# Weights loaded twice, once rounded by GpSimd's transfers, with the remainder formed by VectorE alone

## The chip, the cores and the metric

One core of one Trainium2 chip runs the whole program. The metric is the device time of one execution in microseconds; lower is better. Before the change it is 3626.53 us, the median of three runs (3625.71 to 3627.09).

## The reference, cut to what matters

A stack of two kinds of transformer block on one sequence of 512 tokens with 1024 features, in float32. Two layers of the first kind (Fourier mixing, window attention and memory attention side by side, then a gated feed-forward layer), two of the second (a half-weighted feed-forward layer, a mixer of three branches, a second half-weighted feed-forward layer), and a last norm. The parts that the text speaks of:

```python
def swiglu(x, w1, w2):                        # four layers of it, and two of the first kind's like it
    gu = x @ w1                               # 1024 x 5632
    return (silu(gu[..., :2816]) * gu[..., 2816:]) @ w2

def hybrid_mixer(h, ...):                     # twice
    proj = h @ w_in + b_in                    # 1024 x 5792
    y_a = (rg_lru(conv4(pa1)) * gelu(pa2)) @ lru_w_out
    y_b = mla_branch(cq, ckv, kpe, ...)       # 8 heads of causal attention
    c = pc1 * sigmoid(pc2)
    c = causal_depthwise_conv(c, dw_w, dw_b)  # 31 taps on 512 channels
    y_c = silu(layer_norm(c)) @ conv_w_out + b_out
    return (g0 * y_a + g1 * y_b + g2 * y_c) @ w_out
```

## The kernel before, in words

**Tiles.** Activations lie with features along the 128 partitions and the 512 tokens along the free axis, as tiles `s` of 128 x 512 float32 from one pool of `NSLOT` = 95 slots. Weights come as tiles of 128 x 128; one load brings eight of them (512 KB) into one of `RBUFS` = 3 buffers `raw`. PSUM tiles are named `ps`.

**Three matmuls for one.** To reach float32 accuracy with the fast `fp32r` type, each operand is held as a rounded part and a remainder. `split` (line 727) makes them: `h` is a copy into `fp32r` (the profile's CAST), `l` is the source minus `h` (TENSOR_TENSOR, subtract). `mm3` (line 721) then issues three matmuls. `wload` (line 695) does this for weights: one DMA on SyncE's queue into `raw` (the very first load in two halves, flag `fresh`), and for each four weight tiles one cast and one subtraction of 128 x 512. `wsmall` (line 713) does the same for small weights, in slots.

**Who does what.** `Plan` (line 316) records all instructions in the program's order, simulates the engines with the prices of `price` (line 397) and issues each engine's instructions in the order in which the simulation started them. Some instructions may go to either of two engines, whichever the simulation finds free: `Plan.copy` (line 342) is a copy or cast on ScalarE or VectorE; `Plan.tt` (line 334) is an elementwise operation of two tensors on VectorE or, when no operand is in PSUM, on GpSimd. So weights' casts fall to ScalarE and VectorE, and remainders and other additions and products fall to VectorE and GpSimd. The order on each engine is fixed at build time; at run time each engine waits only on semaphores.

**Stages.** In order: the first block's layer (`block1`, line 1115), its feed-forward layer (`ffn`, line 952), both again; then `ffn`, `mixer` (line 1331), `ffn`, twice. Feed-forward layers are long runs of 128 x 512 matmuls. In `mixer`, `mla` (line 1517) interleaves attention heads with `filler`, which projects the two other branches; `lru` (line 1445) and `dwconv` (line 1486) are elementwise: a `dwconv` is 30 dependent SCALAR_TENSOR_TENSOR instructions on VectorE for each of four tiles, with widths from 511 down to 482, the tap's weight from `vecs`. `conv_norm` (line 1495) adds up the four results and sums over features with a matmul against `onesr`, a tile of ones; the third branch waits for it.

**GpSimd's queue** also issues the DMAs of `fourier` (line 1290), which load the tables `c_dft` into `fp32r` tiles (32 of them, 129 KB each), and computes 17 small powers (`rinv`) for norms. All recorded instructions are issued at line 647, so every row of the profile says L647.

Of the kernel before, what the change touches and what calls it, by code (L numbers as in the profile page):

```python
# [12 lines left out]
F32 = mybir.dt.float32  # L13
# [47 lines left out]
def constants():  # L61
    """Arrays that depend on shapes alone."""
# [63 lines left out]
class Pack:  # L126
    """Vectors along the features, one column for each 128 of them."""
# [114 lines left out]
class View:  # L242
    """A part of a tile that the plan has yet to place."""
# [22 lines left out]
    def box(self):  # L266
        """Partitions and columns that it spans."""
# [10 lines left out]
class Slot:  # L278
    """A tile of the plan: its pool's tag and how long it is needed."""
# [36 lines left out]
class Plan:  # L316
    """Records the instructions in the order of the program, with what each reads and writes, and
    issues them in the order in which the engines could start them: among those that are ready, an
    engine takes the one that the tensor engine needs first."""
# [14 lines left out]
    def tt(self, out, in0, in1, op):  # L334
        """An elementwise instruction that the vector engine or GpSimd may take."""
        kw = dict(out=out, in0=in0, in1=in1, op=op)
        ways = [("vector", "tensor_tensor", (), kw)]
        if not any(v.tile.psum for v in (out, in0, in1)):
            ways.append(("gpsimd", "tensor_tensor", (), kw))
        self.record(ways)  # L340

    def copy(self, out, in_):
        """A copy that the scalar or the vector engine may take."""
        kw = dict(out=out, in_=in_)
        self.record([("scalar", "copy", (), kw), ("vector", "tensor_copy", (), kw)])

    def scale(self, out, in_, by):
        """A product with a column (or a number)."""
# [48 lines left out]
    def price(self, way, outs, ins):  # L397
# [21 lines left out]
        if fn == "dma_start":  # L419
            return 1.0  # L420
# [6 lines left out]
    def schedule(self):  # L427
        """The order of issue and each instruction's engine, by a simulation of the engines."""
# [43 lines left out]
        def room(op, ahead, e):  # L472
            """Whether its tiles fit now, and still would with all before it in the program."""
# [14 lines left out]
        def elsewhere(op, e):  # L488
            """When another engine would have finished it."""
# [59 lines left out]
        while done < len(self.ops):  # L549
            moved = True  # L550
            while moved:
                moved = False
                for e in self.ENGINES:
                    while idle_at[e] <= now + 1e-9 and queues[e]:
# [21 lines left out]
                        elif op.fn == "dma_start":  # L576
                            op.end = now + 4.0
# [73 lines left out]
class Weights:  # L651
    """Tiles of weights, four in each slot."""
# [11 lines left out]
class Net:  # L664
    NSLOT = 95
    RBUFS = 3
# [3 lines left out]
    def __init__(self, plan, I, out, at, nl1=2, nl2=2):  # L670
        self.nc, self.I, self.out, self.at = plan, I, out, at
        self.nl1, self.nl2 = nl1, nl2
        self.fresh = True
# [21 lines left out]
    def wload(self, src):  # L695
        """A load of weights and the split of its tiles of 128 columns."""
# [3 lines left out]
        for c in (0, 4) if self.fresh else (0,):  # L700
            e = c + 4 if self.fresh else n
            nc.sync.dma_start(out=raw[:, c:e], in_=src[:, c:e])
        self.fresh = False
        hs, ls = [], []
        for c in range(0, n, 4):
            e = min(c + 4, n)
            h, l = (self.t(F32R)[:, :128 * (e - c)].rearrange("p (k c) -> p k c", c=128) for _ in range(2))
            self.split(raw[:, c:e], h, l)
# [4 lines left out]
    def wsmall(self, src):  # L713
        """Weights of at most 512 columns, in slots."""
        n = src.shape[1]
        raw, wh, wl = (self.t(dt)[:, :128 * n].rearrange("p (k c) -> p k c", c=128) for dt in (F32, F32R, F32R))
        self.nc.sync.dma_start(out=raw, in_=src)
        self.split(raw, wh, wl)
        return wh, wl
# [22 lines left out]
    def linear(self, srcs, acts, evac, hold=0, before=None, first=0, last=0, done=None):  # L742
        """srcs: for each m tile the pieces of its weights along K. The first hold tiles
        are evacuated after the matmuls of all of them. The first and the last tiles can go by halves
        of the tokens, so that what waits for them or for their operands can begin earlier."""
# [34 lines left out]
    def linear4(self, pairs, acts, evac, only=None):  # L780
        """K = 512, two m tiles for each load."""
# [26 lines left out]
    def norm(self, xs, d, bias=None, wide=False):  # L808
        """1/rms of xs (after their bias) in all partitions."""
# [17 lines left out]
    def wide(self, parts, d):  # L827
        """1/rms in all partitions, from sums of squares; takes less of the tensor engine
        than inv() and bcast() but longer."""
# [784 lines left out]
```

## Time and profile before

| what | us |
|---|---|
| runs of the kernel, median (range) | 3626.53 (3625.71 to 3627.09) |
| the profiled execution, from its first to its last instruction | 3625.2 |
| TensorE (PE) busy | 3460.9 (95%) |
| VectorE (DVE) busy | 2558.2 (71%) |
| ScalarE (ACT) busy | 1008.3 (28%) |
| GpSimd (POOL) busy | 735.2 (20%) |

No time of its own is given for the profiled execution beside its span of 3625.2 us; the median of the runs lies 1.3 us above the span. Busy shares are means over stages that differ: in the feed-forward layers TensorE never pauses, in the mixers VectorE hardly does. The engines' names in the rows are PE, DVE, ACT, POOL and SP (SyncE).

### The profile page before, as it was taken

The numbers are of one execution on the slowest core, as the hardware profiler recorded it, in microseconds if no ns is written. First come the engines' busy times: TensorE is split into PE (matmuls) and PEld (weight loads), VectorE is DVE, ScalarE is ACT, GpSimd is POOL, SyncE is SP. The second block draws the span as 40 slices with busy tenths as digits, with TensorE's granted clock in tenths as the row PEclk, the third lists the DMA queues.
The fourth block names the chain that finished last, engine by engine and source line by source line (L and its number), as shares of the span: only waits on it lengthen the run. The fifth ranks groups of instructions, "written<-read, shape, count | busy, mean of one in ns | idle before, by whom it ended". The sixth has DMA issues, their size and how long they took to land.

```text
span 3625.2 us, 42725 instructions
## 1 busy us (share of the span) xinstructions
PE 3460.9 (95%) x16280; PEld 2874.0 (79%) x16280; DVE 2558.2 (71%) x4377; ACT 1008.3 (28%) x1944; POOL 735.2 (20%) x582
## 2 busy tenths in 40 slices
PE   7999999989999999999995999999999999599998
PEld 6788888778888888887784888888888878488887
DVE  8987545888553865479999765566556999975553
ACT  5632112453110311037523211021102662321110
POOL 4341003443000400013434000000001243510000
PEclk8999999999999999999997999999999999899999
DMA  4223232232223232331222422332233122242231
GB/s 143 81 66 111 82 102 73 81 99 76 82 94 98 81 109 84 103 118 55 93 72 86 139 76 80 108 121 78 80 112 133 42 72 93 81 138 83 80 104 50
DMA packets 105406, 331.61 MB, mean 91 GB/s; under 512 B 12272, under 2 KB 21232, under 8 KB 105200
## 3 DMA queue, kind: packets, MB, share of 16 engines
q1 hardware_dynamic: 100592, 324.64, 27.2%
q0 software_dynamic: 4608, 4.23, 0.5%
q8 instruction: 128, 2.10, 0.2%
q14 instruction: 78, 0.64, 0.1%
HBM read 319.91 MB, written 6.29 MB: 90 GB/s over the span
## 4 chain that ended last, share of the span: by engine, by line
PE 76%; DVE 21%; issue 2%; ACT 1%; DMA 0%; POOL 0%; SPq 0%; DVEq 0%; ACTq 0%; POOLq 0%
PE ps L647 76%; DVE s L647 20%; ACT s L647 1%; DVE nb L647 0%; DMA s<-in_x 0%; DVE mx L647 0%; DMA raw<-in_a_in 0%; DVE sp L647 0%; POOL rinv L647 0%; SPq L647 0%; DVE rc L647 0%; POOL s L647 0%; DVE sums L647 0%; DVE rms L647 0%; DVEq L647 0%
## 5 line engine op out<-in xcount | busy, mean ns | idle before, releaser
L647 PE MATMUL ps<-s 128*128 128x512 f32 (+3 forms) x15706 | 3399.8, 378 | 44.9 <-DVE s L647 36.0
L647 PEld LDWEIGHTS ps<-s 128*128 128x128 f32 (+1 forms) x15706 | 2804.5, 189 | 609.1 <-DVE s L647 50.0
L647 DVE TENSOR_TENSOR s<-ps,s 128x512 f32<-128x512 f32 (+5 forms) x642 | 394.8, 635 | 515.6 <-PE ps L647 512.2
L647 DVE TENSOR_TENSOR s<-raw,s 128x512 fp32r<-128x512 f32 (+1 forms) x918 | 640.1, 719 | 23.4 <-ACT s L647 5.5
L647 POOL TENSOR_TENSOR s<-s 128x512 f32<-128x512 f32 (+2 forms) x277 | 335.1, 1219 | 1526.6 <-DVE s L647 893.2
L647 POOL TENSOR_TENSOR s<-raw,s 128x512 fp32r<-128x512 f32 (+1 forms) x250 | 366.6, 1480 | 1177.0 <-ACT s L647 534.7
L647 ACT ACTIVATE s<-s 128x512 f32<-128x512 f32 (+1 forms) x325 | 182.6, 579 | 1074.6 <-DVE s L647 1041.1
L647 DVE TENSOR_TENSOR s<-s 128x512 f32<-128x512 f32 (+3 forms) x573 | 423.9, 746 | 60.5 <-ACT s L647 35.9
L647 ACT CAST s<-raw 128x512 fp32r<-128x512 f32 (+1 forms) x564 | 326.4, 606 | 434.9 <-DMA raw<-in_b 181.1
L647 DVE SCALAR_TENSOR_TENSOR s<-s,vecs 128x256 fp32r<-128x256 f32 (+25 forms) x446 | 386.2, 897 | 2.8
L647 DVE CAST s<-raw 128x512 fp32r<-128x512 f32 (+1 forms) x604 | 277.9, 466 | 21.2 <-DMA raw<-in_b 10.9
L647 ACT ACTIVATE s<-s,vecs 128x512 f32<-128x512 f32 (+2 forms) x211 | 134.5, 654 | 389.5 <-DVE s L647 354.2
L647 DVE SCALAR_TENSOR_TENSOR s<-ps,s 128x512 f32<-128x512 f32 (+1 forms) x33 | 22.2, 674 | 236.4 <-PE ps L647 236.4
L647 ACT CAST s<-s 128x512 fp32r<-128x512 f32 (+1 forms) x97 | 58.6, 609 | 235.4 <-DVE s L647 183.2
L647 ACT ACT_TABLE_LOAD x68 | 87.2, 1283 | 54.0 <-DVE s L647 52.2
L647 DVE CAST s<-s 128x512 fp32r<-128x512 f32 (+2 forms) x167 | 87.3, 523 | 14.4 <-POOL s L647 10.6
L647 PE MATMUL ps<-ident,s 128*128 128x128 f32 x392 | 65.9, 293 | 31.0 <-DVE s L647 29.0
L647 ACT ACTIVATE s<-ps 128x512 f32<-128x512 f32 (+1 forms) x40 | 21.3, 533 | 235.6 <-PE ps L647 235.5
L647 DVE RECIPROCAL s<-s 128x128 f32<-128x128 f32 (+1 forms) x48 | 83.3, 1742 | 4.2 <-ACT s L647 4.0
L647 PE MATMUL ps<-s,onesr 128*128 128x512 f32 x36 | 13.0, 444 | 76.5 <-DVE s L647 42.3
L647 PEld LDWEIGHTS ps<-ident,s 128*128 128x128 f32 x392 | 49.3, 149 | 46.2 <-DVE s L647 34.2
L647 ACT ACTIVATE s<-s,nb 128x256 f32<-128x256 f32 (+3 forms) x128 | 70.6, 553 | 37.5 <-DVE nb L647 37.3
(61 smaller groups left out, 701.1 us busy)
## 6 DMA issues: line engine op xcount, KB each, us to landing
raw<-in_b SPq DMA_DIRECT2D x240, 512.0 KB, 3.3
raw<-in_a_f SPq DMA_DIRECT2D x120, 512.0 KB, 3.3
raw<-in_b_in SPq DMA_DIRECT2D x92, 512.0 KB, 3.2
raw<-in_b SPq DMA_DIRECT2D x32, 384.0 KB, 3.6
raw<-in_a_in SPq DMA_DIRECT2D x19, 512.0 KB, 4.2
raw<-in_a_out SPq DMA_DIRECT2D x16, 512.0 KB, 3.2
raw<-in_b_out SPq DMA_DIRECT2D x16, 512.0 KB, 3.2
raw<-in_a_f SPq DMA_DIRECT2D x16, 384.0 KB, 3.6
```

Source lines behind the costliest of these rows:

```text
L647: getattr(getattr(nc, op.eng), op.fn)(*[real(v) for v in op.args], **{k: real(v) for k, v in op.kw.items()})
```

## The change

The weights' rounded part no longer comes from a cast on ScalarE or VectorE. A second DMA, on GpSimd's queue, reads the same weights from HBM and writes them into an `fp32r` tile; the DMA converts. The raw weights still arrive on SyncE's queue, and VectorE subtracts. `Plan.tt` no longer offers GpSimd, so every elementwise operation of two tensors is VectorE's; GpSimd keeps the DMAs and the 17 powers. Two slots fewer, one raw buffer more, the first load in one piece, and the planner's prices for GpSimd's DMAs change: they now share the planner's one DMA channel with SyncE's. Since the planner picks the order by its prices, the order changes on every engine.

```diff
@@ class Plan: def tt(self, out, in0, in1, op)
-        kw = dict(out=out, in0=in0, in1=in1, op=op)
-        ways = [("vector", "tensor_tensor", (), kw)]
-        if not any(v.tile.psum for v in (out, in0, in1)):
-            ways.append(("gpsimd", "tensor_tensor", (), kw))
-        self.record(ways)
+        self.record([("vector", "tensor_tensor", (), dict(out=out, in0=in0, in1=in1, op=op))])
@@ price
         if fn == "dma_start":
-            return 1.0
+            return 0.6
@@ schedule
                         elif op.fn == "dma_start":
-                            op.end = now + 4.0
+                            n = int(np.prod(op.kw["out"].shape[1:]))
+                            passes = 2 if "accum_op" in op.kw else 1
+                            state["dma"] = max(state["dma"], now + 1.0) + passes * 128 * n * 4 / 330e3
+                            op.end = state["dma"] + 1.6
@@ class Net
-    NSLOT = 95
-    RBUFS = 3
+    NSLOT = 93
+    RBUFS = 4
@@ wload
-        for c in (0, 4) if self.fresh else (0,):
-            e = c + 4 if self.fresh else n
-            nc.sync.dma_start(out=raw[:, c:e], in_=src[:, c:e])
-        self.fresh = False
+        nc.sync.dma_start(out=raw, in_=src)
         hs, ls = [], []
         for c in range(0, n, 4):
             e = min(c + 4, n)
             h, l = (self.t(F32R)[:, :128 * (e - c)].rearrange("p (k c) -> p k c", c=128) for _ in range(2))
-            self.split(raw[:, c:e], h, l)
+            nc.gpsimd.dma_start(out=h, in_=src[:, c:e])
+            nc.tt(l, raw[:, c:e], h, ALU.subtract)
@@ wsmall
         self.nc.sync.dma_start(out=raw, in_=src)
-        self.split(raw, wh, wl)
-        return wh, wl
+        self.nc.gpsimd.dma_start(out=h, in_=src)
+        self.nc.tt(l, raw, h, ALU.subtract)
+        return h, l
```

How the built programs differ. In the whole program VectorE has 4379 instructions before and 4279 after, ScalarE 1786 and 1214, GpSimd 587 and 1256 (1247 of them DMAs, 1215 of weights), TensorE 16199 in both.

GpSimd's queue in the first mixer, where the second and third branches are computed (`raw` is a weight buffer, `s` a slot), before:

```order
L647 TENSOR_TENSOR s_16391<-raw_16332,s_16384 128x512
L647 TENSOR_TENSOR s_16428<-raw_16332,s_16411 128x512
L647 TENSOR_TENSOR s_16470<-raw_16372,s_16449 128x512
L647 TENSOR_TENSOR s_16533<-raw_16430,s_16509 128x512
L647 TENSOR_TENSOR s_15911<-s_15911,s_16480 128x512
L647 TENSOR_TENSOR s_16562<-raw_16472,s_16555 128x512
```

and of the change (`in_b_mo0`, `in_b_in0` are weights in HBM):

```order
L646 DMA s_15860<-in_b_mo0 128x512
L646 DMA s_15868<-in_b_mo0 128x512
L646 DMA s_15923<-in_b_in0 128x512
L646 DMA s_15940<-in_b_in0 128x512
L646 DMA s_15963<-in_b_in0 128x512
L646 DMA s_15983<-in_b_in0 128x512
```

Remainders and additions have left this queue, and DMAs stand there instead.

VectorE's queue at the end of the first mixer's `dwconv` and the start of `conv_norm`, before:

```order
L647 SCALAR_TENSOR_TENSOR s<-s,vecs 128x483
L647 TENSOR_TENSOR s<-ps,s 128x512
L647 SCALAR_TENSOR_TENSOR s<-s,vecs 128x482
L647 TENSOR_TENSOR s<-s 128x512 x2
L647 TENSOR_TENSOR s<-ps,s 128x512
L647 TENSOR_TENSOR s<-s 128x512
L647 TENSOR_TENSOR s<-raw,s 128x512 x2
```

and of the change:

```order
L646 SCALAR_TENSOR_TENSOR s<-s,vecs 128x483
L646 SCALAR_TENSOR_TENSOR s<-s,vecs 128x482
L646 TENSOR_TENSOR s<-s 128x512 x5
L646 TENSOR_TENSOR s<-raw,s 128x512 x2
L646 TENSOR_TENSOR s<-s 128x512 x13
L646 TENSOR_TENSOR s<-ps,s 128x512
```

The two orders do much the same work around the last tap; between the first SCALAR_TENSOR_TENSOR of `mla` and this last tap VectorE has 508 instructions before and 557 after (76 remainders of weights for 26, 60 other two-tensor operations in SBUF for 37, 55 scalings for 48, no cast of weights for 21, 20 other casts for 31).

TensorE at the same place, before (`onesr` is the tile of ones of `conv_norm`):

```order
L647 MATMUL ps<-s 128x512 x583
L647 MATMUL ps<-s,onesr 128x512 x2
L647 MATMUL ps<-s 128x512 x31
L647 MATMUL ps<-s,onesr 128x512 x2
L647 MATMUL ps<-s 128x512 x535
```

and of the change:

```order
L646 MATMUL ps<-s 128x512 x584
L646 MATMUL ps<-s,onesr 128x512 x2
L646 MATMUL ps<-s 128x512 x23
L646 MATMUL ps<-s,onesr 128x512 x2
L646 MATMUL ps<-s 128x512 x525
```

Counted from the program's start, 8909 matmuls stand ahead of the first `onesr` pair before and 8927 after; in the second mixer 14070 and 14081.

## Rows read from the trace of the kernel before

**Rows 1.** The page: busy time by engine, and the chain by engine.

```profile
PE 3460.9 (95%) x16280; PEld 2874.0 (79%) x16280; DVE 2558.2 (71%) x4377; ACT 1008.3 (28%) x1944; POOL 735.2 (20%) x582
PE 76%; DVE 21%; issue 2%; ACT 1%; DMA 0%; POOL 0%; SPq 0%; DVEq 0%; ACTq 0%; POOLq 0%
```

**Rows 2.** Windows: a feed-forward stretch, first mixer, second mixer, a turn, the start.

```profile
core 0: us, PE busy (x) PEld busy (x) DVE busy (x) ACT busy (x) POOL busy (x), PEclk, DMA share, GB/s
2084.00:2628.00 544.00, 544.00 (x2402) 450.62 (x2401) 308.54 (x529) 80.56 (x135) 25.82 (x18) 1.00 0.28 90
...
1599.00:1933.00 334.00, 295.26 (x1362) 239.54 (x1360) 324.12 (x541) 152.70 (x281) 127.03 (x85) 0.95 0.20 67
2806.00:3137.00 331.00, 294.90 (x1367) 239.33 (x1365) 322.92 (x542) 152.97 (x282) 130.20 (x85) 0.96 0.20 68
...
619.00:663.00 44.00, 38.09 (x233) 34.16 (x233) 41.22 (x54) 17.58 (x38) 27.95 (x26) 0.92 0.37 125
...
0.00:11.00 11.00, 4.32 (x8) 2.38 (x9) 5.72 (x12) 5.67 (x8) 0.20 (x4) 1.00 0.76 241
11.00:53.00 42.00, 33.98 (x144) 27.71 (x143) 41.62 (x51) 22.34 (x39) 23.62 (x18) 0.95 0.50 176
```

**Rows 3.** Timeline of TensorE at `conv_norm`, first and second mixer.

```profile
1936.39 1.22 PE L647 MATMUL ps<-s,onesr 128*128 128x512 f32 x2 [35.26 <-DVE s L647]
...
3141.56 1.22 PE L647 MATMUL ps<-s,onesr 128*128 128x512 f32 x2 [34.22 <-POOL s L647]
```

**Rows 4.** Timeline of 1910 to 1922, VectorE and GpSimd: start, length, instructions.

```profile
1910.50 0.68 DVE L647 TENSOR_TENSOR s<-ps,s 128x512 f32<-128x512 f32 x1
1911.10 9.61 DVE L647 SCALAR_TENSOR_TENSOR s<-s,vecs 128x482 f32<-128x482 f32 x7
1911.95 1.62 POOL L647 TENSOR_TENSOR s<-s 128x512 f32<-128x512 f32 x1 [1.89 <-DVE s L647]
1913.53 1.69 POOL L647 TENSOR_TENSOR s<-raw,s 128x512 fp32r<-128x512 f32 x1
1915.19 1.69 POOL L647 TENSOR_TENSOR s<-s 128x512 f32<-128x512 f32 x1
```

**Rows 5.** VectorE's groups in the first mixer, 1599 to 1933: busy us, mean ns.

```profile
L647 DVE SCALAR_TENSOR_TENSOR s<-s,vecs 128x509 f32<-128x509 f32 (+29 forms) x147 | 138.4, 972 | 0.9
...
L647 DVE TENSOR_TENSOR s<-raw,s 128x512 fp32r<-128x512 f32 x26 | 20.7, 804 | 0.0
L647 DVE TENSOR_TENSOR s<-s 128x512 fp32r<-128x512 f32 (+2 forms) x25 | 19.4, 777 | 0.2
...
L647 DVE SCALAR_TENSOR_TENSOR s<-s 128x512 f32<-128x512 f32 x16 | 14.1, 882 | 0.0
L647 DVE CAST s<-ps 128x384 fp32r<-128x384 f32 (+4 forms) x19 | 10.1, 547 | 3.4 <-PE ps L647 3.2
```

**Rows 6.** The same window by form: two widths of `dwconv` that GpSimd left alone.

```profile
L647 DVE SCALAR_TENSOR_TENSOR s<-s,vecs 128x508 f32<-128x508 f32 x4 | 2.9, 736 | 0.0
...
L647 DVE SCALAR_TENSOR_TENSOR s<-s,vecs 128x484 f32<-128x484 f32 x4 | 2.8, 711 | 0.0
```

**Rows 7.** All instructions on `raw`: duration ns min/median/max.

```profile
L647 DVE TENSOR_TENSOR s<-raw,s x918: 414/684/1785, 5.8 to 3570.6; 128x512 fp32r<-128x512 f32 x175, 128x256 fp32r<-128x256 f32 x9
L647 DVE CAST s<-raw x604: 280/419/1527, 14.0 to 3569.8; 128x512 fp32r<-128x512 f32 x143, 128x256 fp32r<-128x256 f32 x8
...
DMA to landing us min/median/max: 3.0/3.3/7.4
```

**Rows 8.** The converting DMAs of GpSimd's queue today, and the page's queues.

```profile
L647 POOL DMA_DIRECT2D s<-in_c_dft x32: 527/567/755, 157.7 to 770.5; - x32
...
DMA to landing us min/median/max: 2.3/2.6/4.2
...
q1 hardware_dynamic: 100592, 324.64, 27.2%
q0 software_dynamic: 4608, 4.23, 0.5%
```

**Rows 9.** VectorE's groups in the turn 619 to 663.

```profile
L647 DVE TENSOR_TENSOR s<-raw,s 128x512 fp32r<-128x512 f32 x15 | 13.1, 912 | 0.1
L647 DVE SCALAR_TENSOR_TENSOR s<-s,vecs 128x256 fp32r<-128x256 f32 x11 | 9.1, 878 | 0.0
```

**Rows 10.** The chain at the start: the input's last tile.

```profile
4.50 6.77 DMA s<-in_x
```

More of the change, by code (lines that the diff above doesn't have):

```diff
@@ L672, in __init__ @@
         self.nl1, self.nl2 = nl1, nl2
-        self.fresh = True
     def t(self, dt=F32):
@@ L715, in wsmall @@
         n = src.shape[1]
-        raw, wh, wl = (self.t(dt)[:, :128 * n].rearrange("p (k c) -> p k c", c=128) for dt in (F32, F32R, F32R))
+        raw, h, l = (self.t(dt)[:, :128 * n].rearrange("p (k c) -> p k c", c=128) for dt in (F32, F32R, F32R))
         self.nc.sync.dma_start(out=raw, in_=src)
-        self.split(raw, wh, wl)
-        return wh, wl
+        self.nc.gpsimd.dma_start(out=h, in_=src)
+        self.nc.tt(l, raw, h, ALU.subtract)
+        return h, l
     def mm3(self, ps, wh, wl, ah, al, start, stop, **k):
```

## The prediction

> **What bounds the kernel now.** I read the page first: TensorE is busy 95% of the span and carries 76% of the chain, VectorE 21% [rows 1]. The windows then separate the stages [rows 2]. In the feed-forward stretch TensorE is busy all 544 us, 2402 matmuls at 226 ns; VectorE is busy 57% of it, GpSimd 26 us. Nothing that VectorE, ScalarE or GpSimd save there can shorten the run. In the two mixers it is the other way round: VectorE is busy 324.1 of 334 us and 322.9 of 331 us (97%), while TensorE stands 39 and 36 us. The timeline shows where: ahead of the `onesr` matmul of `conv_norm` TensorE waits 35.3 us in the first mixer and 34.2 us in the second [rows 3], for the end of the depthwise convolution and the sum over it. The second of these waits is ended by a GpSimd instruction. So the change is worth what it does to VectorE in the mixers, plus the few turns between stages where VectorE is also full (41.2 of 44 us, [rows 2]).
>
> **What the reader should see next: GpSimd slows VectorE.** From 1911.95 on GpSimd runs its two-tensor instructions back to back, and beside them seven convolution taps of VectorE take 9.61 us, 1.37 us each [rows 4]; taps that GpSimd left alone take 711 to 736 ns [rows 6]. A remainder has a median of 684 ns and a maximum of 1785 ns; a cast 419 and 1527 ns [rows 7]. An instruction of VectorE that meets one on GpSimd thus loses about what it takes itself. GpSimd is busy 127 and 130 us in the mixers [rows 2].
>
> **The sum, part by part.**
>
> *Mixers, what goes.* In the first mixer 147 taps and the like average 972 ns; at 730 ns (between the two rows of [rows 6]) that is 147 x 0.242 = 35.6 us less. 26 remainders at 804 against 684: 3.1. 25 other two-tensor operations at 777 against 684: 2.3. 16 of SCALAR_TENSOR_TENSOR on slots at 882 against 684 (taken from the remainder, also two tensors in SBUF): 3.2. These four groups [rows 5, 6, 7] give 44 us; the smaller groups I leave out as a reserve.
>
> *Mixers, what comes.* By the order, up to the last tap VectorE has 50 remainders and 23 other two-tensor operations more, 73 x 0.684 = 49.9 us; one more evacuation, 0.7; 7 scalings at about a cast's 0.419, 2.9. It has 21 casts of weights less, 8.8 us; 2 other SBUF casts less, 0.8; 9 casts out of PSUM less at 0.547 [rows 5], 4.9. Net 39.0 us.
>
> So VectorE reaches the last tap 5 us earlier. The order also puts 18 matmuls more (11 in the second mixer) ahead of the wait; at 0.226 us they are 4.1 and 2.5 us of TensorE's standing time filled. I take 9 and 8 us: **17 us for both mixers**. The second is taken as the first's mirror, its VectorE and GpSimd times differing by 1% and 2% [rows 2].
>
> *Turns.* At 619 to 663, 15 remainders average 912 ns and 11 half-width splits 878 [rows 9]; at 684 and half a tap's width, say 475, they lose 3.4 + 4.4 us, and the smaller groups about as much again. The order gives this turn 15 instructions more on VectorE, 6 to 7 us after the casts that go. I take **7 us** for this turn and, since TensorE stands little at the two later turns into feed-forward layers, 3 us for those together.
>
> *Casts and ScalarE.* ScalarE loses its weights' casts and is busy 28% [rows 1]: nothing on the path. In feed-forward layers VectorE loses about 85 casts and gains some 10 to 40 two-tensor operations per layer: hidden under TensorE; if that cover went, it would be a gain of some us.
>
> *DMA traffic.* The rounded copies are 536 loads of 512 KB, 48 of 384 KB and 6 MB of small ones, 306 MB. At SyncE's rate (27.2% for 324.64 MB) they add 26% of the 16 DMA engines, at the present converting DMAs' rate (0.5% for 4.23 MB, rows of half the length) 36% [rows 8]: 53 to 63% in all. Hidden: 24 matmuls take 5.4 us, and that is the time for one raw load and two copies.
>
> *GpSimd's queue.* 1247 DMAs x 0.567 us = 707 us [rows 8], as busy as today, one copy per 2.7 us needed. In the order each copy waits for the copy eight places ahead, so eight may be under way; at 4.2 us of landing, the slowest seen, that allows one per 0.5 us. The 17 powers stand in the same queue behind copies that wait for a free slot; I cost that at nothing, since the slots come free in the order in which TensorE uses them, with the bound in the third rival.
>
> *Start.* The input's last tile lands at 11.3 us [rows 10] at 241 GB/s with DMA 76% busy [rows 2]. The copies begin at once on the other queue: between 0 and a doubling of that 6.8 us. Against it, VectorE, full from 11 to 53 us (41.6 of 42, [rows 2]), loses GpSimd's company (23.6 us busy) and has 45 instead of 55 instructions up to the first evacuation. But TensorE has 89 instead of 140 matmuls by then. I take 0 within -8 and +12.
>
> Sum: 17 + 7 + 3 + 0 = 27, and 8 for the groups left out as a reserve in the two mixers (5 casts, scalings and additions each that sit beside GpSimd, and `conv_norm` itself, 20 of whose 28 us have GpSimd beside them): **35 us**. The execution read has a span of 3625.2 us; the runs' median is 1.3 above. 3626.5 - 35 = **3592 us**. Its own range, from half to one and a half times the gain: 3570 to 3612.
>
> **A rule against it.** The converting DMAs of today took 527 to 755 ns to issue and 2.3 to 4.2 us to land while VectorE worked beside them [rows 8], so the sum prices no hold-up. The Trainium skill (SBUF — State Buffer, "A bandwidth-pool intuition that's wrong" and "Who interferes with whom") says that a DMA issued by GpSimd cannot write its descriptors while VectorE copies or casts in its two-port mode, about 3.1 us instead of 0.62. No run so far shows that length. By it, an estimate: if one in ten of 102 copies per mixer met such an instruction and lost 2.5 us on VectorE's path, 50 us in all, the result would be 3642 instead of 3592.
>
> **Rivals.**
>
> 1. *More than forecast, 3555.* All of TensorE's standing in the mixers that is above what the fill needs goes: half of 39 + 36 us. For it: 130 us of GpSimd beside VectorE may cost more than my four groups say. Against: 39 us of new work per mixer.
> 2. *No gain, 3626.* VectorE stays the bound of the mixers, and the 39 us that come equal what goes, because its instructions are slowed by the descriptors' writing as they were by arithmetic, or the start takes the gain back. For it: the margin of the mixers is only 5 us of 330. Against: operations beside today's 32 DMAs kept their usual length.
> 3. *Slower: the copy comes after its remainder's turn, 3670.* VectorE works in order, and each remainder now waits for two transfers, one of them issued by a queue whose head may wait for a slot. Everything behind it on VectorE, taps too, waits along. The place is the mixers, where VectorE has no slack. A landing spreads by 1.6 us on GpSimd's queue and 4.1 us on SyncE's (median to maximum, [rows 7, 8]). If 19 of the 76 remainders came 2 us late, that is 38 us per mixer: 3592 + 76 = 3668. It decides from about 9 us of such waits per mixer on, since the gain there is 9. For it: only 2.6 to 3.3 us separate issue from use at best, and twice the bytes share 16 engines. Against: the DMA engines are 20% busy in the mixers [rows 2], and copies can be issued long ahead.
> 4. *VectorE's own work holds GpSimd's issue up, 3656.* The place is the 102 copies of each mixer: a copy whose issue meets a cast or a scaling of VectorE lands late. Today's landings spread from 2.6 to 4.2 us, 1.6 us [rows 8]; if one copy in five comes so much later on VectorE's path, 20 x 1.6 = 32 us per mixer, 64 in all: 3592 + 64 = 3656. For it: VectorE is busy 97% there, so that most issues have something beside them. Against: the longest issue of today is 755 ns, and the weights' casts leave VectorE. This is the Trainium skill's rule named above, at a price from rows.
>
> **How the numbers follow.** A measurement of this kernel can tell 0.2%, 7 us, from no change. Chances: forecast 0.48, rival 1 0.09, rival 2 0.13, rival 3 0.23, rival 4 0.07. Faster is the forecast and rival 1, 0.57; same is rival 2, 0.13; slower rivals 3 and 4, 0.30. The range for 8 in 10 runs from 3548, which takes in most of rival 1, to 3690, which takes in rival 4 and rival 3 up to some 24 late copies per mixer.
>
> **What the changed profile would show.** Right: VectorE's remainders at 684 ns and its taps at 711 to 736 ns throughout the mixers; GpSimd without two-tensor rows but the powers; the wait ahead of `onesr` at 20 to 28 us; feed-forward stretches still without a pause of TensorE; DMA share near 0.55 there. Wrong, if VectorE's idle time in the mixers is ended by DMAs into `s` or `raw`, if TensorE pauses in a feed-forward layer, or if the remainders stay near 800 ns with GpSimd doing no arithmetic.

## The result, and the profile after

The changed kernel takes **3589.18 us** (median of 4 runs, 3586.07 to 3589.67); the kernel before took 3626.81 in the same session. The ratio is 0.9895 with a 95% interval of 0.9881 to 0.9909: faster by 37.6 us, 33 to 43 by the interval. 3592 had been forecast. The profiled execution has a span of 3587.8 us against 3625.2, and 37.4 us less is what has to be found in the rows.

The page after, busy times by engine and the chain by engine (answers to [rows 1]):

```profile
PE 3463.5 (97%) x16280; PEld 2874.5 (80%) x16280; DVE 2312.7 (64%) x4277; ACT 699.4 (19%) x1372; POOL 671.1 (19%) x1251
PE 87%; DVE 10%; issue 1%; DMA 1%; ACT 0%; SPq 0%; POOL 0%; POOLq 0%; DVEq 0%; ACTq 0%
```

TensorE's work is what it was (2.6 us more); 40 us of its standing are gone, and VectorE's share of the chain falls from 21% to 10%. VectorE is busy 245 us less, though it has only 100 instructions fewer and these are no shorter on the whole: 604 casts of raw weights went, and 527 two-tensor operations came from GpSimd. The fall is time that instructions no longer lose.

The windows of [rows 2], over the same times, after (the changed kernel enters the two mixers 21 and 31 us earlier, so its rows there reach further into the work):

```profile
core 0: us, PE busy (x) PEld busy (x) DVE busy (x) ACT busy (x) POOL busy (x), PEclk, DMA share, GB/s
2084.00:2628.00 544.00, 544.00 (x2402) 450.46 (x2401) 261.48 (x421) 37.96 (x59) 104.90 (x199) 1.00 0.61 185
1599.00:1933.00 334.00, 300.67 (x1363) 245.36 (x1362) 322.75 (x612) 126.81 (x228) 58.99 (x110) 0.94 0.52 154
2806.00:3137.00 331.00, 296.99 (x1351) 242.83 (x1350) 319.57 (x593) 124.49 (x220) 59.90 (x112) 0.95 0.55 166
619.00:663.00 44.00, 43.69 (x287) 40.02 (x286) 41.02 (x83) 11.14 (x28) 12.36 (x24) 1.00 0.91 281
0.00:11.00 11.00, 2.79 (x5) 1.50 (x6) 5.29 (x11) 3.26 (x4) 6.20 (x15) 1.00 0.86 256
11.00:53.00 42.00, 32.99 (x118) 24.82 (x117) 31.32 (x51) 11.41 (x17) 12.71 (x23) 0.80 1.09 349
```

The feed-forward stretch is still without a pause, at a DMA share of 0.61 instead of 0.28. In the mixers VectorE is as full as before (97%), but runs 612 instructions where 541 ran. At the turn it runs 83 instead of 54, and TensorE 287 matmuls instead of 233. The last row has turned the other way: from 11 to 53 us the DMA engines are full, VectorE idles for a quarter, and TensorE has 118 matmuls instead of 144.

VectorE's groups in the first mixer, after (lines, busy us and mean ns; answers to [rows 5]):

```profile
L646 DVE SCALAR_TENSOR_TENSOR s<-s,vecs 128x511 f32<-128x511 f32 (+23 forms) x140 | 96.6, 729 | 0.7
...
L646 DVE TENSOR_TENSOR s<-raw,s 128x512 fp32r<-128x512 f32 x88 | 58.2, 681 | 0.0
L646 DVE TENSOR_TENSOR s<-s 128x512 fp32r<-128x512 f32 (+2 forms) x73 | 47.1, 672 | 0.5
...
L646 DVE SCALAR_TENSOR_TENSOR s<-s 128x512 f32<-128x512 f32 x16 | 10.9, 684 | 0.3 <-ACT s L646 0.2
```

Taps 729 ns instead of 972, remainders 681 instead of 804, other two-tensor operations 672 instead of 777, the last group 684 instead of 882. And no remainder of the whole run is slowed any more. All instructions of VectorE on `raw` (count, then ns min/median/max), where [rows 7] had 684 with a maximum of 1785:

```profile
L646 DVE TENSOR_TENSOR s<-raw,s x1168: 414/683/694, 7.5 to 3534.1; 128x512 fp32r<-128x512 f32 x195
```

At the turn of 619 to 663, the two groups of [rows 9] that took 912 and 878 ns:

```profile
L646 DVE TENSOR_TENSOR s<-raw,s 128x512 fp32r<-128x512 f32 x17 | 10.8, 682 | 0.0
L646 DVE SCALAR_TENSOR_TENSOR s<-s,vecs 128x256 fp32r<-128x256 f32 x15 | 6.5, 476 | 0.0
```

The copies of GpSimd's queue, the largest group and the one with the longest issue (ns min/median/max), and the page's two load queues ([rows 8]):

```profile
L646 POOL DMA_DIRECT2D s<-in_b x544: 527/528/652, 1140.1 to 3526.5; - x182
...
L646 POOL DMA_DIRECT2D s<-in_a_mk x8: 527/532/807, 24.8 to 149.6; - x8
```

```profile
q0 software_dynamic: 176832, 310.49, 30.9%
q1 hardware_dynamic: 100448, 324.64, 27.0%
```

TensorE's pauses at `conv_norm` in the first mixer, after (timeline of TensorE; the last bracket is the idle time ahead and who ended it):

```profile
1883.40 6.97 PE L646 MATMUL ps<-s 128*128 128x512 f32 x18 [10.65 <-DVE s L646]
...
1898.38 1.22 PE L646 MATMUL ps<-s,onesr 128*128 128x512 f32 x2 [6.43 <-DVE s L646]
...
1907.64 0.73 PE L646 MATMUL ps<-s,onesr 128*128 128x512 f32 x2 [1.34 <-DVE s L646]
...
1920.77 4.63 PE L646 MATMUL ps<-s 128*128 128x512 f32 x10 [11.93 <-DVE s L646]
```

The 35.3 us wait of [rows 3] is 6.4 now, but two others have come beside it: the 10.65 and the 11.93 us above. In the second mixer the three are 14.48, 3.16 and 11.94 us.

**Where the 37 us come from.** TensorE executes 16280 matmuls in either kernel. I take from each trace the start of the 1250th, 5000th, 7500th, 9500th and 14500th (counted from 0; all in feed-forward layers, where TensorE never pauses, so the order of single matmuls doesn't matter) and of the last. The table gives, for each stretch between two of them, its length less that of the kernel before, in us; the kernels of the experiments stand beside. Each column is one execution. How far single ones differ shows in e7, which has the changed kernel's order on VectorE, ScalarE and GpSimd up to the first mixer and yet gains 4.8 us more in the second attention block.

| stretch | changed | e1 | e3 | e5 | e9 | e6 | e7 | e2 | e10 | e8 | e11 |
|---|---|---|---|---|---|---|---|---|---|---|---|
| start, to 259 us before | +2.1 | -17.6 | -14.2 | -10.7 | -13.8 | -7.3 | +2.5 | +23.7 | -16.7 | -14.8 | -22.0 |
| second attention block, to 1036 | -17.7 | -17.2 | -25.1 | -16.9 | -16.9 | -17.1 | -22.5 | +7.7 | -16.6 | -25.1 | -9.0 |
| turn at 1194 to 1233, to 1573 | -4.9 | -5.1 | -4.9 | -5.0 | -5.0 | -5.0 | -4.9 | -0.5 | -3.0 | -4.9 | -4.9 |
| first mixer, to 2063 | -10.9 | -10.5 | -8.2 | -10.8 | -10.8 | -2.2 | -24.6 | +13.0 | +21.8 | -51.8 | -51.8 |
| second mixer, to 3227 | -5.6 | -5.3 | -2.8 | -5.5 | -5.5 | +4.1 | -19.0 | +22.0 | +27.9 | -46.1 | -46.0 |
| all, to the last matmul | -37.1 | -55.9 | -55.3 | -49.2 | -52.3 | -27.7 | -68.8 | +65.9 | +13.1 | -142.6 | -133.9 |

For the changed kernel: the second attention block gives most, the mixers 16.5, and the start takes 2.1. What the runs had to tell is whether GpSimd's arithmetic is the cause (A), or the casts that left the other engines (B), or the second transfer (C), and what goes on at the start (D or E).

### The profile page after: what moved, and what is told of

Read it like the earlier page. It is cut to its first block, busy times and chain, and to the rows that moved or that the text cites. A ratio compares the mean times of both kernels' runs of the same rounds, so it can differ in the third digit from the quotient of the medians.

```text
span 3587.8 us, 43800 instructions
## 1 busy us (share of the span) xinstructions
PE 3463.5 (97%) x16280; PEld 2874.5 (80%) x16280; DVE 2312.7 (64%) x4277; ACT 699.4 (19%) x1372; POOL 671.1 (19%) x1251
## 4 chain that ended last, share of the span: by engine, by line
PE 87%; DVE 10%; issue 1%; DMA 1%; ACT 0%; SPq 0%; POOL 0%; POOLq 0%; DVEq 0%; ACTq 0%
PE ps L646 87%; DVE s L646 10%; ACT s L646 0%; DMA s<-in_pos 0%; DMA s<-in_x 0%; DVE sp L646 0%; SPq L646 0%; ACT L646 0%; DVE nb L646 0%; DVE mx L646 0%; DVE rc L646 0%; POOLq L1594 0%; POOL rinv L646 0%; DVE rms L646 0%; POOL s L646 0%
## 5 line engine op out<-in xcount | busy, mean ns | idle before, releaser
L646 PE MATMUL ps<-s 128*128 128x512 f32 (+4 forms) x15706 | 3406.6, 378 | 99.1 <-DVE s L646 88.1
L646 PEld LDWEIGHTS ps<-s 128*128 128x128 f32 (+2 forms) x15706 | 2805.1, 189 | 672.8 <-DVE s L646 105.7
L646 DVE TENSOR_TENSOR s<-ps,s 128x512 f32<-128x512 f32 (+4 forms) x642 | 397.7, 636 | 639.5 <-PE ps L646 634.1
L646 DVE TENSOR_TENSOR s<-raw,s 128x512 fp32r<-128x512 f32 (+1 forms) x1168 | 736.7, 672 | 59.5 <-DMA raw<-in_b 13.7
L646 DVE TENSOR_TENSOR s<-s 128x512 f32<-128x512 f32 (+3 forms) x850 | 515.2, 624 | 44.4 <-ACT s L646 22.1
L646 POOL DMA_DIRECT2D s<-in_b x544 | 287.5, 534 | 1302.1 <-PE ps L646 940.0
L646 DVE SCALAR_TENSOR_TENSOR s<-s,vecs 128x256 fp32r<-128x256 f32 (+25 forms) x446 | 286.6, 677 | 2.8 <-ACT s L646 0.4
L646 POOL DMA_DIRECT2D s<-in_a_f x272 | 144.2, 538 | 561.0 <-PE ps L646 385.7
L646 POOL DMA_DIRECT2D s<-in_b_in x184 | 99.2, 541 | 396.5 <-PE ps L646 310.7
L646 ACT CAST s<-ps 128x256 fp32r<-128x256 f32 (+4 forms) x154 | 66.2, 458 | 89.9 <-PE ps L646 73.6
```

The lines of the kernel that those rows point to most:

```text
L646: getattr(getattr(nc, op.eng), op.fn)(*[real(v) for v in op.args], **{k: real(v) for k, v in op.kw.items()})
```

## The experiments

Each ratio is against the kernel before in the same session.

**e1_vector_only.** The kernel before, with GpSimd's arithmetic taken away and nothing else:

```diff
-        ways = [("vector", "tensor_tensor", (), kw)]
-        if not any(v.tile.psum for v in (out, in0, in1)):
-            ways.append(("gpsimd", "tensor_tensor", (), kw))
-        self.record(ways)
+        self.record([("vector", "tensor_tensor", (), kw)])
```

> The kernel before with one edit: two-tensor operations have VectorE as their only engine. Weights are still loaded once and cast by ScalarE or VectorE, so no second transfer exists. Theory A (the change gains because GpSimd's two-tensor instructions stop slowing VectorE): VectorE's remainders come down to 684 ns and its taps to about 730 ns. Up to the last tap of a mixer its instructions sum to 372 us at the durations they have beside an idle GpSimd, 10 more than in the changed kernel (362) and some 12 less than the 332 plus 52 of slowing in the kernel before. So 3589 + 2 x 10, and a few us in the turns: 3612 us, between 3600 and 3622. Theory B (the gain comes from the casts that leave VectorE and ScalarE, whoever does the arithmetic): VectorE gets 411 instructions more and loses none, 40 us more per mixer, and the time is 3690 us or so; anything above 3640 speaks for B.

Measured: 3570.67 us, ratio 0.9847 (0.9834 to 0.9860). B is out: VectorE has 411 instructions more than before, and the kernel is 56 us faster. A's side, but 41 us below its point and outside its range: this one edit gives more than the whole change. Three groups of VectorE in the first mixer (lines, 1599 to 1933):

```profile
L644 DVE SCALAR_TENSOR_TENSOR s<-s,vecs 128x510 f32<-128x510 f32 (+26 forms) x136 | 93.3, 728 | 0.7
L644 DVE TENSOR_TENSOR s<-raw,s 128x512 fp32r<-128x512 f32 x99 | 65.1, 682 | 0.2
...
L644 DVE TENSOR_TENSOR s<-s 128x512 f32<-128x512 f32 (+1 forms) x72 | 47.0, 678 | 0.6
```

And its window of 11 to 53, where the changed kernel's VectorE idled and its DMA share was 1.09:

```profile
11.00:53.00 42.00, 36.47 (x158) 29.75 (x157) 40.06 (x70) 20.20 (x35) 0.00 (x0) 0.96 0.48 162
```

The durations are those of the changed kernel. By the table it gains what the changed kernel gains in every stretch, to within 0.5 us, but for the start, where it is 19.7 us ahead. So the second transfer, with the edits beside it (slots, buffers, the planner's prices), brings nothing over the old casts anywhere and costs 19.7 us at the start. My 20 us for 372 instead of 362 us of VectorE's work in the two mixers did not show: in the traces VectorE's instructions from the 7500th matmul to the first mixer's last tap sum to 364.2 us in e1 and 364.1 in the changed kernel, and that tap ends 343.3 and 343.5 us after the matmul.

**e3_scalar_cast.** The changed kernel without the second transfer; ScalarE casts:

```diff
-            nc.gpsimd.dma_start(out=h, in_=src[:, c:e])
+            nc.scalar.copy(h, raw[:, c:e])
...
-        self.nc.gpsimd.dma_start(out=h, in_=src)
+        self.nc.scalar.copy(h, raw)
```

> The changed kernel with one edit in the two loaders: the rounded weights are cast from raw by ScalarE alone, and no second transfer is made. GpSimd's queue keeps its 32 transfers and the powers. Theory A (what counts is VectorE's work and that GpSimd does no arithmetic; the second transfer only takes casts off engines that have room): VectorE sums to 367 us in each mixer, 5 more than the changed kernel, and the start is spared the traffic, 2 us by 260 us: 3597 us, between 3588 and 3605. Theory C (the second transfer is what makes it pay, because a remainder then waits for two loads side by side and not for a load, a cast and ScalarE's queue): remainders wait for ScalarE, VectorE idles in the mixers for over 10 us each, and the time is 3615 us or more.

Measured: 3571.47 us, 0.9847 (0.9834 to 0.9861). C is out, and my 3597 was too slow: I had put 2 us on the start, which gained 16.3, and nothing on the second attention block, which gained 7.4. ScalarE is busy 1321.6 us here, 37% of the span, so the casts have room there. The whole time can't be told apart from e1's, though e3 has the edits beside the second transfer and e1 has not. By the table, e3 is 2.7 and 2.8 us behind the changed kernel in the mixers, so there the second transfer gives a little over casts by ScalarE alone.

**e2_gpsimd_back.** The changed kernel with `Plan.tt` as before the change (the removed lines of e1's diff put back); the copies stay.

> The changed kernel with one edit: GpSimd may take two-tensor operations again; the rounded copies stay on its queue. VectorE's instructions up to the last tap of a mixer sum to 316 and 321 us instead of 362. Theory A: GpSimd takes 461 of them, against 527 in the kernel before, and slows VectorE by about 52 x 461/527 = 45 us per mixer, which gives the 44 us back; remainders average about 800 ns again, and the copies queue behind arithmetic: 3595 to 3630 us, 3605 the likeliest. Theory B (GpSimd's arithmetic is free help for VectorE): some 40 us per mixer less, up to the 30 us for which TensorE stands there: 3530 to 3560 us.

Measured: 3684.56 us, 1.0159 (1.0145 to 1.0173). A's side, but 80 us above its likeliest value and outside its range; the five runs spread from 3678.00 to 3693.92, and the rows are from the longest. VectorE's groups in the first mixer:

```profile
L650 DVE SCALAR_TENSOR_TENSOR s<-s,vecs 128x509 f32<-128x509 f32 (+28 forms) x115 | 97.1, 876 | 3.3 <-ACT s L650 2.7
...
L650 DVE TENSOR_TENSOR s<-raw,s 128x512 fp32r<-128x512 f32 x38 | 32.1, 853 | 2.9 <-DMA s<-in_b_in 2.9
```

From its table of waits (engine, what it waited for, us in total, times, longest):

```profile
DVE s L650 <- DMA s<-in_a_f: 63.9, 39, 3.5
POOL s L650 <- DMA raw<-in_b: 44.7, 6, 10.5
...
POOL s L650 <- DMA raw<-in_b_lo: 24.7, 3, 13.2
```

The slowing is back (876 and 853 ns), and something new with it: GpSimd stands up to 13 us in front of a remainder whose raw weights have not landed, with copies queued behind it. VectorE's waits for copies grow too, from 12.7 to 63.9 us for `in_a_f`, but 58.7 of these lie between 261 and 620 and between 860 and 1250 us, mostly feed-forward layers; in the two mixers they are 8.5 and 3.9 us, for 9.5 and 3.1 in the changed kernel. So copies do come late here, as in the third rival, but that they cost anything is not shown. How the 80 us divide between the slowing and the blocked queue I did not separate.

**e5_start16 and e9_start40.** The changed kernel; the first 16 (40) loads are cast by ScalarE instead of loaded twice:

```diff
-            nc.gpsimd.dma_start(out=h, in_=src[:, c:e])
+            if self.loads < 16:
+                nc.scalar.copy(h, raw[:, c:e])
+            else:
+                nc.gpsimd.dma_start(out=h, in_=src[:, c:e])
```

> The changed kernel with one edit: the first 16 loads of weights have their rounded part cast by ScalarE instead of loaded a second time (32 of 1215 copies fewer). In the changed kernel the DMA engines are over 90% busy from 0 to 45 us (116% and 117% from 15 to 45), the 100th matmul starts 14.0 us later than before the change, and the stretch up to the first feed-forward layer is 2.1 us behind. Theory D (the copies that run ahead crowd out the input and the first weights): the DMA share from 15 to 45 us falls below 0.9, the 100th matmul comes at about 36 us instead of 47.7, and the entry into the feed-forward layer is 3 to 9 us earlier: 3580 to 3586 us. Theory E (the start is bound by VectorE and the chain through it, and the traffic is beside it): no change beyond 2 us, 3587 to 3591 us.

> The changed kernel with the first 40 loads of weights (all of the first attention block and part of its feed-forward layers) cast by ScalarE instead of loaded a second time; with 16 it took 3577.7 us. Theory A (away from the start the second transfer costs and gives nothing: in every later stretch the changed, the vector-only and the ScalarE-cast kernels gain the same within 1 us): 3571 us, between 3568 and 3575. If the copies cost something later as well, it stays at 3576 to 3578 us.

Measured: 3577.66 us, 0.9865 (0.9852 to 0.9878), and 3573.77 us, 0.9855 (0.9842 to 0.9869). D holds, and e5 gains more than D's range gave it (3580 to 3586); e9 lies in its range. The window of 15 to 45 us in the changed kernel, then in e5 (columns as above):

```profile
15.00:45.00 30.00, 21.79 (x76) 17.07 (x76) 24.76 (x40) 8.57 (x13) 11.13 (x20) 0.72 1.16 389
```

```profile
15.00:45.00 30.00, 30.00 (x135) 24.82 (x134) 27.48 (x46) 19.17 (x34) 3.48 (x6) 1.00 0.64 220
```

The DMA share falls from 1.16 to 0.64, TensorE has no pause left where it stood 8.2 us, and the 100th matmul (counted from 0) starts at 33.8 instead of 47.7. The granted clock tells the same: 0.72 of full speed on average in the changed kernel, a mix of the levels of 1.2 and 2.4 GHz behind TensorE's pauses (0.50, which is 1.2 GHz, from 20 to 35 us), 1.00 (2.4 GHz throughout) in e5. What was late stands in the changed kernel's chain of 0 to 100 us: the last tile of the input takes 9.52 us to land, 6.77 before ([rows 10]), and the positions 11.62 us behind it (at most 5.5 before):

```profile
4.82 9.52 DMA s<-in_x
14.36 11.62 DMA s<-in_pos
```

With 40 loads the start gains 15.9 against the changed kernel, and all later stretches stay within 0.8 us of it. e9's remaining 2 to 3 us to e1 and e3 lie inside the intervals.

**e6_lead25.** All copies stay, but none is planned over 25 us ahead of its use:

```diff
+            nc.lead = 25.0
             nc.gpsimd.dma_start(out=h, in_=src[:, c:e])
+            nc.lead = nc.AHEAD
```

> The changed kernel with one edit: a rounded copy may be planned at most 25 us before TensorE needs it, instead of 120 us; nothing else about the copies changes, and all 1215 stay. Theory D1 (the start is lost because copies that nobody needs yet run ahead of the input and the first weights): the DMA share from 15 to 45 us falls from 1.16 to below 0.9 and most of the 19.7 us by which the start of the changed kernel stands behind the vector-only kernel comes back: 3570 to 3580 us. Theory D2 (the first layers need both transfers of their weights at the rate at which they come, so no order of them helps): 3585 to 3592 us. If copies that start only 25 us ahead come late, VectorE waits for transfers into the slots in the mixers too, and the time is above 3592.

Measured: 3598.97 us, 0.9923 (0.9909 to 0.9936): outside D1's and D2's ranges; it lies where late copies were expected, but not for that cause. The table splits it. The start is 9.4 us better than the changed kernel's (DMA share 0.83 from 15 to 45 us), about half of what crowding cost, where D1 wanted most of it. Yet the 100th matmul still starts at 46.1 us: thirteen copies are issued by 13.6 us as in the changed kernel, and the lead holds back only later ones. So what is lost up to there seems lost to copies that are needed early, which is nearer to D2. Against this the entry into each mixer loses: between the 7500th and the 8000th matmul 13.4 us, in the second mixer about as much. TensorE waits there 6.48 us for ScalarE, behind VectorE's instructions, at 1586.13, and at 1570 to 1610 has 116 matmuls where the changed kernel has 177 (granted clock 0.83 and 1.00). VectorE's waits for copies are not longer than in the changed kernel (10.5 us on `in_a_f` and 2.3 on `in_b_in`, for 12.7 and 12.5), so this is another order of issue and not late landings. Which step of the planner makes it, I leave open.

**e7_taps.** The price of VectorE's time in a mixer; 20 taps left out in each:

```diff
-        for d in range(1, 31):
+        for d in range(1, 26):
```

> The changed kernel with 5 of the 31 taps of the depthwise convolution left out, 20 instructions of VectorE or 20 x 0.73 = 14.6 us in each mixer; the output lacks them. Theory A (VectorE's sum sets the length of the mixers): TensorE's standing time there falls by as much, 3589 - 29 = 3560 us, between 3556 and 3568. Theory F (the remaining 31 and 32 us of TensorE's standing time are the chain of conv_norm behind the last tap, not VectorE's work): less than 8 us, 3581 us or more.

Measured: 3562.37 us, 0.9822 (0.9809 to 0.9836), 26.8 us below the changed kernel. The mixers give 13.7 and 13.4 us for 14.6 us of instructions: in a mixer of the changed kernel, 0.93 us of the run hang on each us of VectorE. F is out.

**e10_idle_arith.** The suspected cost by itself: e1 with one slot fewer, and useless products on GpSimd, recorded beside the taps, which nothing reads:

```diff
             self.stt(c[:, :T - d], w(30 - d), acc[:, d:], ALU.mult, ALU.add, out=acc[:, d:])
+            if d % 2 == 0:
+                nc.gpsimd.tensor_tensor(out=self.junk, in0=c, in1=c, op=ALU.mult)
```

> The suspected cost by itself: the vector-only kernel (3570.7 us), whose VectorE keeps its work, with 60 useless two-tensor products on GpSimd in each mixer, one for every second tap of the depthwise convolution, into a tile of their own that nothing reads (one slot fewer for it). Theory A (a two-tensor instruction of GpSimd slows VectorE beside it): in the kernel before, 85 instructions of GpSimd and 127 us of them cost VectorE 52 us per mixer, 0.61 to 0.65 us each; 60 x 0.65 = 39 us, of which 0.93 reaches the end as with the taps left out (26.8 us for 2 x 14.6), 4 us for the other order: 3571 + 2 x 40 = 3651 us, between 3630 and 3665, with taps beside them near 1.4 us instead of 0.73. Theory B (GpSimd's arithmetic costs VectorE nothing, and the vector-only kernel gained in another way): 3568 to 3580 us.

Measured: 3638.64 us, 1.0034 (1.0022 to 1.0047), 68 us above e1. The mixers are 32.3 and 33.2 us longer, and no other stretch by more than 2.1. Each product costs 0.55 us at the end of the run, for 1.4 us of GpSimd's own. The planner let the 60 of the first mixer run in three bursts, from 1623.91, 1763.45 and 1792.64 us, so they meet only some of the taps and other instructions as well. All products (the tile `junk`, ns min/median/max):

```profile
L644 POOL TENSOR_TENSOR junk<-s x120: 1038/1366/2858, 1623.9 to 3000.8; 128x512 f32<-128x512 f32 x120
```

One width of the taps in the first mixer (lines by form):

```profile
L644 DVE SCALAR_TENSOR_TENSOR s<-s,vecs 128x511 f32<-128x511 f32 x8 | 8.2, 1026 | 0.0
```

Three groups there, one with both operands in SBUF, one with an operand in PSUM, and one with a single operand in SBUF (lines); then the last one in e1:

```profile
L644 DVE TENSOR_TENSOR s<-raw,s 128x512 fp32r<-128x512 f32 x78 | 58.9, 775 | 0.1
L644 DVE TENSOR_TENSOR s<-ps,s 128x512 f32<-128x512 f32 (+5 forms) x92 | 54.0, 613 | 1.8 <-PE ps L644 1.6
...
L644 DVE CAST s<-raw 128x512 fp32r<-128x512 f32 x21 | 15.1, 737 | 0.0
```

```profile
L644 DVE CAST s<-raw 128x512 fp32r<-128x512 f32 x21 | 8.6, 416 | 0.0
```

Taps of 511 columns take 1026 ns instead of 735 in e1 (their whole group 795 instead of 728), remainders 775 instead of 682, while operations with one operand in PSUM stay at 613 (616 in e1). Casts of raw weights, which have one operand, are slowed as well, from 416 to 737 ns, and so are scalings in SBUF (the profile's TENSOR_SCALAR `s<-s`), from 419 to 611. This shows A as a cause: VectorE's own work is e1's but for the planner's small shifts, and only idle arithmetic was added. An estimate, from each instruction's time less the median of its form in the kernels without GpSimd's arithmetic: VectorE loses 32.4 and 33.6 us in the two mixers, what the mixers grow by, and some 11 and 10 us of it fall on casts and scalings. The Trainium skill (SBUF — State Buffer, "Who interferes with whom") states that a VectorE instruction with two inputs in SBUF contends with one of GpSimd that reads SBUF, and that one with at most one such input does not, unless it is in a two-port mode, which copies, casts and `tensor_scalar` can enter; these rows agree.

**e8_accum and e11_accum_more.** If VectorE is the bound of the mixers, its remainders should go elsewhere. In e8 ScalarE casts as in e3, and for the mixers' large weights (a flag set around `mixer`) it also writes minus the rounded part, onto which a transfer adds the raw weights; e11 sets the flag in the attention blocks too, but for the first 10 loads.

```diff
-            nc.gpsimd.dma_start(out=h, in_=src[:, c:e])
-            nc.tt(l, raw[:, c:e], h, ALU.subtract)
+            nc.scalar.copy(h, raw[:, c:e])
+            if self.acc:
+                nc.scalar.activation(out=l, in_=h, func=AF.Identity, scale=-1.0)
+                nc.gpsimd.dma_start(out=l, in_=src[:, c:e], accum_op=ALU.add)
+            else:
+                nc.tt(l, raw[:, c:e], h, ALU.subtract)
```

> The kernel with casts by ScalarE alone (3571 us), and in the mixers the remainders of the large weights leave VectorE too: ScalarE writes minus the rounded part, and a transfer of GpSimd's queue adds the raw weights onto it (276 such transfers). VectorE's sum up to the last tap falls from 367 to 306 us per mixer. Theory A (VectorE's sum sets the mixers): TensorE's standing time of 33 us per mixer falls to the 12 us or so of the chain behind the last tap: 3571 - 42 = 3529 us, between 3515 and 3545. If the adding transfers land late or slow VectorE, as a rival would have it, remainders arrive after TensorE needs them and the time is 3565 us or more.

> The kernel with adding transfers (3484.5 us) with these also in the two attention blocks, but for the first 10 loads of the program, which stay as they are. VectorE is full there too (47 of 50 us from 100 to 150). VectorE has 54 remainders fewer. Theory A: of 54 x 0.684 = 37 us on VectorE, some half lies on the path before the turn into the feed-forward layers, where TensorE still stands 20 us behind the first load and 10 in the turn at 600 to 860: 3470 to 3482 us. If the longer way of a remainder (load, cast, minus, adding transfer) is late where layers follow closely, 3485 to 3500 us.

Measured: e8 **3484.51 us**, 0.9610 (0.9597 to 0.9624), the fastest of all, 105 us below the changed kernel; e11 3492.76, 0.9630 (0.9617 to 0.9643). e8's busy times on the page:

```profile
PE 3432.9 (99%) x16280; PEld 2861.3 (82%) x16280; DVE 2171.9 (62%) x4042; ACT 1463.6 (42%) x2802; POOL 263.1 (8%) x319
```

Its windows over the times of [rows 2] for the mixers (e8 enters the two mixers 45 and 97 us earlier):

```profile
1599.00:1933.00 334.00, 332.63 (x1525) 273.32 (x1524) 282.28 (x500) 239.37 (x421) 93.12 (x109) 1.00 0.80 184
2806.00:3137.00 331.00, 330.65 (x1495) 272.75 (x1494) 269.12 (x450) 214.05 (x373) 81.87 (x96) 1.00 0.78 188
```

The largest group of its adding transfers (issue, ns min/median/max):

```profile
L646 POOL DMA_DIRECT2D s<-in_b_in x184: 847/855/1194, 1475.8 to 3023.6; - x184
```

TensorE stands 1.4 and 0.4 us in the two windows where it stood 39 and 36. Over the same work, from the 7500th to the 9500th and from the 12500th to the 14500th matmul, it stands 1.4 us each, for 46.3 and 43.5 before and 33.3 and 34.2 in the changed kernel. The time lies 31 us below the range: I had kept 12 us per mixer for the chain behind the last tap, and it vanished too. By the first mixer's last tap 8939 matmuls have started, 8996 in the changed kernel, so more were left to fill the chain. There are 264 adding transfers, not the 276 of the expectation. e11 misses theory A's range. In the first attention block it gains 7.2 us more than e8, and in the second it loses 16.1; TensorE stands 2.11 us for an `in_a_in` transfer at 602.70, and the DMA share from 600 to 640 is 1.08. That the longer way of a remainder is late where layers follow closely fits, but I did not test it apart.

## Why the prediction was right, and where it was not

**The cause** holds, and is shown by e1 and e10: two-tensor instructions of GpSimd slow VectorE's operations on two SBUF operands, and its casts and scalings in SBUF too. The group durations came out as taken: taps 729 ns (730 taken), remainders 681 (684), other two-tensor operations 672 (684).

**The sum** came out at 37 for 35, but not by its terms, so that the total fits so well is luck. (Half to one and a half times 35 us is 3574 to 3609, not the 3570 to 3612 that I wrote; the result lies in both.)

- *Mixers*: 17 and a reserve of 8 were taken; the table has 10.9 and 5.6, 16.5 together. Up to the last tap the gain was put too low: counted from the 7500th (12500th) matmul it ends 18.0 (15.7) us earlier than before, where 5 were taken, and by the estimate made for e10 VectorE's instructions had lost 51 (53) us by then, for 44 taken. Behind it the gain was put too high: from the last tap to the end of the stretch the changed kernel is 7.1 (10.1) us longer. Before, 59 matmuls stood ready behind the first mixer's second `onesr` pair, and then TensorE waited 2.4 us; now 2 stand ready, and it waits 11.93. So the steps that failed are that what is won ahead of the wait was counted as won for the run, that a reserve was put on top for `conv_norm`, and that the second mixer was taken as the first's mirror: it gives half.
- *Turns*: 10 were taken, 22.6 came (17.7 and 4.9). I costed the window of 619 to 663 alone, where VectorE was full, and took the rest of that block as little. The mechanism was right and the size was off: between the 2876th and the 3251st matmul (606 to 680 us before) 14.3 us are gained where 7 were taken, and in the turn into the next feed-forward layer (823 to 866) 8.4 more, with 5.0 lost in between. TensorE's waits for VectorE in the block fall from 25.2 to 13.7 us.
- *Start*: 0 within -8 and +12 was taken, +2.1 came, and the agreement is an accident. The step that failed is VectorE losing GpSimd's company: without copies it is worth 17.6 us here (e1), a third of e1's gain. The copies' traffic, put at 0 to 6.8 us by the landing of the input, costs 16.3 (by e3, which differs in the second transfer alone) to 19.7 (by e1). I looked at the input's last tile; the copies, which only the landing of earlier copies held back, ran ahead of the positions as well.
- *Casts, feed-forward layers, GpSimd's queue*: costed at nothing, and so it is: no pause in a feed-forward layer, and away from the start the changed kernel and e1 agree within 0.5 us. DMA share 0.61, for 53 to 63% taken; the copies took 528 ns to issue in the median, for 567 taken. There are 1196 copies in the trace, not 1215, and 1228 DMAs of GpSimd, not 1247: my counts took in 19 small computations of GpSimd.

**The rivals.** Less than the first rival came. The second, no gain because writing descriptors slows VectorE as arithmetic did, is refuted by 1196 copies beside remainders that never took over 694 ns. The third, late copies, took nothing measurable away from the start: VectorE's longest wait for a copy in the changed kernel is 3.1 us, and its waits on `in_b_in` copies sum to 12.5 us over the run; the mixers still take what they take in e1, which has no copies. The fourth, issue held up by VectorE, is not seen: 128 of GpSimd's 1228 issues run beside a cast or scaling of VectorE in SBUF, with a median of 530 ns (528 for the rest), and the longest of all took 807 ns. No run here shows the 3.1 us that the Trainium skill gives (SBUF — State Buffer, "A bandwidth-pool intuition that's wrong"), though casts and scalings were still running on VectorE.

**The signs** to look for: remainders, taps, GpSimd without arithmetic, and feed-forward layers came as named. The wait ahead of `onesr` did not: 6.4 us (3.2 in the second mixer) and not 20 to 28, since two waits beside it took 10.65 and 11.93.

## What to carry to other kernels

Before an idle engine is given arithmetic, ask what it shares with the bound one: here GpSimd's help cost VectorE more than it took off it, and taking it away, one short edit, gave 56 us. A second transfer that is free in the steady state has its price at the start, where everything lands at once; look at the DMA share of the first 50 us apart, and give the early loads the old way. When stages have different bounds, compare the kernels stretch by stretch at points where the bound engine never pauses: a sum that comes out right may be made of terms that do not.

## What the runs showed that was not expected

- The start was worth as much as the second attention block: 17.6 us gained by e1, and 16 to 20 lost to traffic in the changed kernel.
- The same two edits do not add up: GpSimd's arithmetic alone costs 56 us (before against e1), and with copies in its queue 95 (e2 against the changed kernel).
- An adding transfer of 256 KB took 855 ns to issue in the median (a converting one 528), and 264 of them, with two instructions of ScalarE for each, took 87 us off e3, the largest gain of all single edits here.
